# S5 tables issued behind the first half of the FFN with a narrower scratch, and two mixer gates issued before the NSA heads, in a two-block transformer kernel

## Chip, cores and metric

One core of one Trainium2 chip runs the whole program in one launch. The metric is the device time of one execution in microseconds (us), the median of several runs. Besides, one execution is recorded by the hardware profiler; its span is the time from the first to the last instruction.

## What is computed

Two transformer blocks in fp32 on 256 tokens of width 1024. Cut to what matters here:

```
first_block:                                   # x_lat [256, 1024]
    h = modulate(rmsnorm(x), shift, scale)     # shift, scale: silu(c) @ w_ada, a GEMV
    x = x + g_a * (two attentions of h) @ w_out
    h = modulate(rmsnorm(x), sh_f, sc_f)
    gate, up = split(h @ w_ffn_in, 2)          # FFN hidden 2816
    x = x + g_f * ((silu(gate) * up) @ w_ffn_out)
    x = rmsnorm(x)
second_block:
    hp = rmsnorm(x) @ w_in_2                   # u | q | kv | nsa gates | two mixer gates of 1024
    y_ssm = s5_mixer(u)                        # complex diagonal scan over 32 groups x 64 states
    y_nsa = nsa_mixer(q, kv)                   # compressed + selected + window attention, 8 heads
    merged = sigmoid(gate0) * (y_ssm @ w_proj_ssm) + sigmoid(gate1) * (y_nsa @ w_proj_nsa)
    x = x + merged @ w_out_2
    x = x + square(relu(rmsnorm(x) @ w_up)) @ w_down
s5_mixer: abar = exp(a*dt); bbar = f(abar) * b; x_t = abar * x_(t-1) + bbar u_t
          y = Re(c x) + d u;  yg = gelu(y);  out = yg * sigmoid(yg @ w_glu + b_glu)
```

Rotating the states by the phase of abar turns the complex scan into real ones. That needs cos and sin of every phase times every step: these are the tables of this study. They depend on the parameters alone, not on x.

## The kernel before, in words

**Products.** Activations lie transposed, `[128 channels, 256 tokens]` a tile, so a weight tile of 128x128 is the stationary operand and 256 (or 258) tokens stream. A product in fp32 accuracy is made of three fp32r matmuls: high part of the weight with the high part of the activation, high with low, and low with high. Weights come as `raw` buffers of 1024 KB by SP's DMA, in the order in which the program uses them; there are three such buffers, each of two halves of 128x1024. For each half ScalarE (ACT) copies `raw` to `hi`, then VectorE (DVE) makes `lo = raw - hi`. TensorE (PE) thus needs one ACT and one DVE instruction for each 24 matmuls (8 tiles times 3). `hi` and `lo` have four buffers each.

**Who orders the work.** Every operation is recorded by the class `Rec` and none is issued at once; all show line 660 (`Rec.issue`) in the profile, so the rows are read by tile names. `schedule()` is a planner with its own costs that fixes the order of the instructions of each engine; its priority is the index in the program plus `rec.shift`. An operation recorded while `rec.gate` holds another one can't be placed before that one has ended. Hardware semaphores do the rest: each engine works through its fixed order and waits where an operand isn't ready.

**FFN, first half (`ffi`).** The loop `for j in range(22)` makes for each `z` of 0, 1 a group of 24 matmuls into one PSUM bank (tags `mm` and `s` in turn), 44 groups in all, 22 pairs. A reading on DVE (`c<-mm,k_rsf` or `c<-s,k_rsf`, 128x258) and small operations follow each group; a pair ends in `hid[j]`, which is split into high and low by ACT and DVE. At j = 2, 6, 10, 14 a `gemv` (a piece of the next adaptive-norm product, `raw<-raw,k_crow`) runs on DVE and GpSimd (POOL) and keeps one `raw` buffer meanwhile. At j = 7 `s5_params()` is recorded: all S5 parameters, complex products of 128x512 and 128x256 on POOL (`c<-c,k_fr`, `k_neg`, `k_abr`, `k_abi`) and, at its end, `tables()`.

**The tables.** `tables()` writes cos and sin of 16 groups of phases for 128 steps by doubling: at level n it squares the phase (small operations of 128x16) and fills columns n to 2n from columns 0 to n by six POOL operations (three pairs: `tab<-tab,col`, `c<-tab,col`, `tab<-tab,c`), in pieces of as many groups as fit in the scratch. The scratch was `c2()`, 512 columns. First use is in the S5 scan (`c<-v,tab`) far behind.

**FFN, second half (`ffo`).** For each of 8 output tiles 66 matmuls over the 22 `hid` tiles; DVE adds the residual, splits and squares.

**Second block.** `site(name)` calls stand all along it and place pieces of other work between its own: `S5_AT` says how many steps of the S5 scan, `GATE_AT` how many mixer gates. One `gate_step()` makes one 256-wide mixer gate, two groups of 24 matmuls (`mm<-xs`), so 48 matmuls, two `hi`, two `lo`, two ACT copies and two POOL multiplications by `r12`. Seven gates are to be done before the GLU (`GATES_A`); those that the sites don't place are recorded after the last S5 steps. Site `c` stands after the compressed keys and values (`k_kcn`, `k_vcn`) and before the scores with them (`s<-k_crow,k_kcn`); `h11`, `h12`, `h13` stand behind the head pairs 1 to 3 of the second query tile, `p10` behind its first value product. Query tile 0 has 128 keys, tile 1 has 256.

Of the kernel before, what the change touches and what calls it, by code (L numbers as in the profile page):

```python
# [202 lines left out]


S5P_AT = 7
S5A_SHIFT = 600
HI_SHIFT = 30
LO_SHIFT = -30
# [5 lines left out]
POOL_A, POOL_B, POOL_N = (1,), (0,), (0, 1)  # L214

S5_AT = {"k0": 1, "k1": 1, "v": 1, "q0": 4, "q2": 1, "c": 3, "h01": 1, "h03": 2, "h13": 1}
GATE_AT = {"h11": 2, "h12": 1, "h13": 2, "p10": 1}

GEMV_AT = {"v0": (0, 1), "v2": (2, 3), "a1": (4,), "a3": (5, 6), "h0": (7,), "h1": (8, 9), "h3": (10, 11)}
GEMV_POOL = [(1,)] * 3 + [()] + [(1,)] * 2 + [(0, 1)] * 3 + [()] + [(0, 1)] * 2 + [(1,), (), (1,), (1,)]  # L220
# [452 lines left out]
def _build(ctx, tc, nc, A, out):  # L673
# [5 lines left out]
    rec = Rec(nc, BUFS)  # L679
# [11 lines left out]
    def T(tag, shape, dt=F32):  # L691
        cnt[0] += 1
        name = f"{tag}_{cnt[0]}"
        return own(sp, name, tag, shape, dt)
# [7 lines left out]
    def PS(tag, shape):  # L702
        cnt[0] += 1
        name = f"{tag}_{cnt[0]}"
        return own(pp, name, tag, shape, F32)
# [16 lines left out]
    def c1(dt=F32, n=256):  # L722
        return T("c1", [128, n], dt)

    def c2(dt=F32):
        return T("c2", [128, 512], dt)
# [8 lines left out]
    def col(name, j=0, n=1):  # L735
        a = PC[name][0]
        return pc[:, a + j:a + j + n]
# [54 lines left out]

    rec.shift = S5A_SHIFT
    ar, ai = col("ar", 0, 16), col("ai", 0, 16)
# [573 lines left out]


    def s5_params():  # L1370
        rec.gate = {hid[0].root.w[-1]}
        ACT.activation(e1, th2, AF.Sin)

        are, den, t0 = cols16(), cols16(), cols16()
        V.tensor_tensor(abr, mag, e1[:, 0], OP.mult)
        V.tensor_tensor(aim, mag, e1[:, 1], OP.mult)
        V.tensor_tensor(mag2, mag, mag, OP.mult)
        V.tensor_scalar(are, abr, 1.0, None, op0=OP.subtract)
        V.tensor_tensor(den, ar, ar, OP.mult)
        V.tensor_tensor(t0, ai, ai, OP.mult)  # L1380
        V.tensor_tensor(den, den, t0, OP.add)
        V.reciprocal(den, den)
        V.tensor_tensor(fr, are, ar, OP.mult)
        V.tensor_tensor(t0, aim, ai, OP.mult)
        V.tensor_tensor(fr, fr, t0, OP.add)
        V.tensor_tensor(fr, fr, den, OP.mult)
        V.tensor_tensor(fi, aim, ar, OP.mult)
        V.tensor_tensor(t0, are, ai, OP.mult)
        V.tensor_tensor(fi, fi, t0, OP.subtract)
        V.tensor_tensor(fi, fi, den, OP.mult)  # L1390
        V.tensor_scalar(neg[:, 0], fi, -1.0, None, op0=OP.mult)
        V.tensor_scalar(neg[:, 1], aim, -1.0, None, op0=OP.mult)
        t16 = lambda: c2().rearrange("p (a b) -> p a b", a=16)
        scm = [t16(), t16()]

        nbt = [[c2().rearrange("p (a m b) -> p a m b", a=8, m=2) for _ in range(2)] for _ in range(2)]
        scd = A["sc"].rearrange("p (a b c) -> p a b c", a=16, b=2)
        for k in range(2):
            SP.dma_start(scm[k], scd[:, :, k])
            for i in range(2):  # L1400
                o = 512 * k + 256 * i
                SP.dma_start(nbt[k][i][:, :, 1], A["sbn"][:, o:o + 256].rearrange("p (a b) -> p a b", a=8))
        ct = t16()
        frb, nfb, arb, aib, nab = (f_[:, :, None].to_broadcast([128, 16, 32]) for f_ in (fr, neg[:, 0], abr, aim, neg[:, 1]))

        def cmul(o, x, yr, yi, op0, op1, ct=ct):

            G.tensor_tensor(o[0], x[0], yr, OP.mult)
            G.tensor_tensor(ct, x[1], yi, OP.mult)
            G.tensor_tensor(o[0], o[0], ct, op0)  # L1410
            G.tensor_tensor(o[1], x[0], yi, OP.mult)
            G.tensor_tensor(ct, x[1], yr, OP.mult)
            G.tensor_tensor(o[1], o[1], ct, op1)


        cp, ca = [t16(), t16()], [t16(), t16()]
        cmul(cp, scm, frb, nfb, OP.add, OP.subtract)

        cmul(ca, cp, arb, nab, OP.subtract, OP.add)
        sb2 = [[c2() for _ in range(2)] for _ in range(2)]  # L1420
        for i in range(2):
            a8 = slice(8 * i, 8 * i + 8)
            o, x = [nbt[k][i][:, :, 0] for k in range(2)], [nbt[k][i][:, :, 1] for k in range(2)]
            cmul(o, x, arb[:, a8], aib[:, a8], OP.subtract, OP.add, ct[:, a8])
            for k in range(2):
                tp = PS("tp", [128, 512])
                for p in range(4):
                    PE.transpose(tp[:, 128 * p:128 * p + 128], nbt[k][i][:, 2 * p:2 * p + 2], ident)
                ACT.activation(sb2[k][i], tp, AF.Copy)

        dd, gd = c2().rearrange("p (a b) -> p a b", a=4), c2().rearrange("p (a b) -> p a b", a=4)
        G.memset(gd, 0.0)
        for q in range(4):
            G.tensor_scalar(dd[:, q], ident, col("ssd", q), None, op0=OP.mult)
        gp = PS("tp", [128, 4, 32])
        for q in range(4):
            for k in range(2):
                for z in range(4):
                    mm(gp[32 * z:32 * z + 32, q], nbt[k][q // 2][:, (4 * q + z) % 8, 1], cp[k][:, 4 * q + z], k == 0, k == 1)
        for z in range(4):  # L1440
            r = slice(32 * z, 32 * z + 32)
            V.tensor_tensor(gd[r, :, r], gp[r], dd[r, :, r], OP.add)


        TB = [T("tab", [128, 16, 128]) for _ in range(2)]

        def tables():
            tc_, ts_ = TB
            e2 = T("col", [128, 2, 16, 1])
            tm = T("col", [128, 16, 1])  # L1450
            pr1, pi1 = e2[:, 0], e2[:, 1]

            def square(c_, s_):
                G.tensor_tensor(pr1, c_, c_, OP.mult)
                G.tensor_tensor(tm, s_, s_, OP.mult)
                G.tensor_tensor(pr1, pr1, tm, OP.subtract)
                G.tensor_tensor(pi1, c_, s_, OP.mult)
                G.tensor_scalar(pi1, pi1, 2.0, None, op0=OP.mult)
            G.memset(tc_[:, :, 0:1], 1.0)
            G.memset(ts_[:, :, 0:1], 0.0)  # L1460
            square(e1[:, 0][:, :, None], e1[:, 1][:, :, None])
            G.tensor_copy(tc_[:, :, 1:2], pr1)
            G.tensor_copy(ts_[:, :, 1:2], pi1)
            t_ = c2()
            for lv in range(1, 7):
                n = 2 ** lv
                h_ = n // 2
                square(tc_[:, :, h_:h_ + 1], ts_[:, :, h_:h_ + 1])
                nj = min(16, 512 // n)
                for j in range(0, 16, nj):  # L1470
                    j_ = slice(j, j + nj)
                    pr, pi_ = (p[:, j_].to_broadcast([128, nj, n]) for p in (pr1, pi1))
                    t = t_[:, 0:nj * n].rearrange("p (a b) -> p a b", a=nj)
                    c_, s_, cn, sn = tc_[:, j_, 0:n], ts_[:, j_, 0:n], tc_[:, j_, n:2 * n], ts_[:, j_, n:2 * n]
                    G.tensor_tensor(cn, c_, pr, OP.mult)
                    G.tensor_tensor(t, s_, pi_, OP.mult)
                    G.tensor_tensor(cn, cn, t, OP.subtract)
                    G.tensor_tensor(sn, s_, pr, OP.mult)
                    G.tensor_tensor(t, c_, pi_, OP.mult)
                    G.tensor_tensor(sn, sn, t, OP.add)  # L1480
        tables()
        rec.gate = set()
        return sb2, cp, ca, dd, gd, TB

    hid = []
    xh_ = lambda kc: xs[kc][:, 256:514]
    xl_ = lambda kc: xs[kc][:, 0:256]
    for j in range(22):
        ts = []
        for z in range(2):  # L1490
            ps = PSR([128, 258], LIN)
            lin(ps, BASE["ffi"] + 16 * j + 8 * z, 8, xh_, xl_)
            t = T("c258", [128, 258])
            V.tensor_tensor(t, ps, rsf, OP.mult)
            V.tensor_scalar(t[:, 256:257], t[:, 257:258], t[:, 256:257], None, op0=OP.add)
            ts.append(t)
        a = c1()
        ACT.activation(a, ts[0][:, 0:256], AF.Silu, bias=ts[0][:, 256:257])
        V.scalar_tensor_tensor(a, ts[1][:, 0:256], ts[1][:, 256:257], a, op0=OP.add, op1=OP.mult)
        h_ = c2(F32R)  # L1500
        split(h_[:, 0:256], h_[:, 256:512], a)
        hid.append(h_)
        if j in (2, 6, 10, 14):
            gemv(12 + j // 4)
        if j == S5P_AT:
            sb2, cp, ca, dd, gd, TB = s5_params()

    gg = K("gg", [128, 8])
    V.tensor_tensor(gg, col("fin", 0, 8), col("n1", 0, 8), OP.mult)
# [130 lines left out]
    def site(name):  # L1640

        s5_step(S5_AT.get(name, 0))
        for _ in range(GATE_AT.get(name, 0)):
            gate_step()
# [268 lines left out]
    hid = []  # L1913
# [10 lines left out]
    for m in range(8):  # L1924
        ps = PSR([128, 256], LIN)
        lin(ps, BASE["down"] + 32 * m, 32, lambda kc: hid[kc][:, 0:256], lambda kc: hid[kc][:, 256:512])
        t_ = c1()
        for z in range(2 if m == 7 else 1):
            c = slice(128 * z, 128 * z + 128) if m == 7 else slice(0, 256)
# [19 lines left out]
```

## Time and profile before

| what | value |
|---|---|
| median of 3 runs | 803.56 us (801.42 to 803.92) |
| profiled execution, time | 800.42 us |
| profiled execution, span | 798.4 us, mean granted clock 0.985 |
| PE busy | 761.0 us, 95% of the span |
| DVE, ACT, POOL busy | 582.9, 432.4, 303.5 us |

The span is 2.0 us shorter than that execution's time, and that execution is 3.1 us below the median of the runs. PE is the engine with the least idle time; how busy the others are changes from stage to stage, so a share of the whole span says little about a stage. In the views, `[1.53 <-DVE lo L660]` behind a row means that the engine was idle for 1.53 us before it and that a `lo` on DVE ended the wait. A group such as `x24` stands for consecutive instructions of one kind.

### The profile page before, as it was taken

The page shows a single profiled execution, that of the slowest core. Times are in us where ns is not written, and L with a number is a line of the kernel's source. Part 1 is how long each engine was busy: PE and PEld are TensorE (multiplying, and loading weights), DVE is VectorE, ACT ScalarE, POOL GpSimd, SP SyncE. Part 2 cuts the span into 40 slices and gives each one's busy share as a digit, 9 for nine tenths or more (in the row PEclk, how much of TensorE's full clock was granted, in tenths as well). Part 3 has the DMA queues.
Part 4 walks back from the last instruction along what each step waited for, and adds up shares of the span by engine and source line. Part 5 has one row for each costly group of instructions (what it writes and reads, how often), then busy time and mean ns, then how long its engine had stood idle before and what let it go on. Part 6 is the DMA issues. An engine that isn't in the chain of part 4 may idle for free.

```text
span 798.4 us, 15427 instructions
## 1 busy us (share of the span) xinstructions
PE 761.0 (95%) x6063; PEld 688.7 (86%) x6063; DVE 582.9 (73%) x1156; ACT 432.4 (54%) x790; POOL 303.5 (38%) x320
## 2 busy tenths in 40 slices
PE   5998999999999898899999988999999999999997
PEld 3877875568999898889999876687999999999997
DVE  6668988787997799866677788756788655555552
ACT  5435559887754445445555323486647666654331
POOL 0013355771368959800002476685350233310000
PEclk9999999999999999999999996999999999999999
DMA  9955543445786454465576401233455555555540
GB/s 329 346 209 223 211 158 114 144 147 218 199 277 214 155 212 159 159 219 203 208 271 205 136 5 53 68 117 135 148 177 205 182 188 188 182 199 192 218 172 14
DMA packets 33994, 142.89 MB, mean 179 GB/s; under 512 B 11777, under 2 KB 15233, under 8 KB 17794
## 3 DMA queue, kind: packets, MB, share of 16 engines
q1 hardware_dynamic: 33922, 141.91, 51.0%
q8 instruction: 48, 0.79, 0.4%
q14 instruction: 24, 0.20, 0.1%
HBM read 139.53 MB, written 1.05 MB: 176 GB/s over the span
## 4 chain that ended last, share of the span: by engine, by line
PE 82%; DVE 9%; DMA 2%; ACT 2%; POOL 2%; issue 1%; SPq 0%; DVEq 0%; POOLq 0%; ACTq 0%
PE mm L660 39%; PE s L660 31%; PE tp L660 6%; DVE c L660 5%; PE la L660 4%; PE v L660 3%; DVE lo L660 3%; DMA raw<-in_ada 1%; ACT c L660 1%; DMA raw<-in_wseq 1%; DVE col L660 1%; ACT hi L660 1%; POOL c L660 1%; POOL tab L660 0%; POOL col L660 0%
## 5 line engine op out<-in xcount | busy, mean ns | idle before, releaser
L660 DVE TENSOR_TENSOR lo<-raw,hi 128x1024 fp32r<-128x1024 f32 x206 | 259.8, 1265 | 92.7 <-ACT hi L660 91.5
L660 ACT ACTIVATE hi<-raw 128x1024 fp32r<-128x1024 f32 x206 | 215.7, 1051 | 194.1 <-PE mm L660 92.4
L660 PE MATMUL mm<-xs,hi 128*128 128x256 f32 (+1 forms) x992 | 185.0, 285 | 2.3 <-ACT hi L660 1.2
L660 PEld LDWEIGHTS mm<-xs,hi 128*128 128x128 f32 x992 | 153.2, 189 | 7.3 <-issue 3.4
L660 PE MATMUL mm<-c,hi 128*128 128x256 f32 (+1 forms) x744 | 140.3, 287 | 4.7 <-DVE c L660 2.7
L660 PE MATMUL mm<-xs,lo 128*128 128x256 f32 (+1 forms) x496 | 140.7, 284 | 2.0 <-DVE lo L660 2.0
L660 PEld LDWEIGHTS mm<-c,hi 128*128 128x128 f32 x744 | 113.7, 188 | 13.8 <-DVE c L660 4.4
L660 PE MATMUL s<-xs,hi 128*128 128x256 f32 (+1 forms) x672 | 125.2, 286 | 0.0
L660 PE MATMUL s<-c,hi 128*128 128x256 f32 (+1 forms) x676 | 120.6, 280 | 1.1 <-ACT hi L660 1.1
L660 PE MATMUL mm<-c,lo 128*128 128x256 f32 (+1 forms) x372 | 105.3, 284 | 1.3 <-DVE lo L660 1.2
L660 PEld LDWEIGHTS s<-c,hi 128*128 128x128 f32 x676 | 103.5, 188 | 2.7 <-ACT hi L660 1.3
L660 PEld LDWEIGHTS s<-xs,hi 128*128 128x128 f32 x672 | 104.8, 191 | 0.5
L660 PE MATMUL s<-xs,lo 128*128 128x258 f32 (+1 forms) x336 | 95.9, 285 | 5.0 <-DVE lo L660 5.0
L660 PEld LDWEIGHTS mm<-xs,lo 128*128 128x128 f32 x496 | 93.8, 189 | 4.3 <-DVE lo L660 2.6
L660 PE MATMUL s<-c,lo 128*128 128x256 f32 x338 | 94.2, 279 | 0.0
L660 ACT ACTIVATE c<-c 128x256 fp32r<-128x256 f32 (+4 forms) x141 | 61.5, 448 | 52.0 <-DVE c L660 48.9
L660 POOL TENSOR_TENSOR raw<-raw,k_crow 128x1024 f32<-128x1024 f32 x18 | 46.2, 2566 | 108.7 <-DMA raw<-in_ada 100.9
L660 DVE TENSOR_TENSOR c<-c,c 128x256 fp32r<-128x256 f32 (+2 forms) x115 | 67.3, 598 | 19.8 <-POOL c L660 15.7
L660 POOL TENSOR_TENSOR c<-c 128x256 f32<-128x256 f32 x40 | 41.6, 1039 | 92.6 <-ACT c L660 80.9
L660 PEld LDWEIGHTS mm<-c,lo 128*128 128x128 f32 x372 | 69.7, 188 | 3.1 <-DVE lo L660 1.7
L660 PEld LDWEIGHTS s<-xs,lo 128*128 128x128 f32 x336 | 64.3, 191 | 6.1 <-DVE lo L660 6.0
L660 PEld LDWEIGHTS s<-c,lo 128*128 128x128 f32 x338 | 63.5, 188 | 0.4
(257 smaller groups left out, 1140.9 us busy)
## 6 DMA issues: line engine op xcount, KB each, us to landing
raw<-in_wseq SPq DMA_DIRECT2D x102, 1024.0 KB, 4.9
raw<-in_ada SPq DMA_DIRECT2D x20, 1024.0 KB, 5.1
tab<-in_ada SPq DMA_DIRECT2D x4, 1024.0 KB, 7.1
c<-in_w SPq DMA_DIRECT2D x8, 256.0 KB, 8.6
k_X<-in_x SPq DMA_DIRECT2D x4, 256.0 KB, 4.1
raw<-in_wseq SPq DMA_DIRECT2D x2, 512.0 KB, 8.0
tab<-in_ctx SPq DMA_DIRECT2D x4, 256.0 KB, 10.5
out<-c SPq DMA_DIRECT2D x7, 128.0 KB, 1.7
```

Of the source, the lines that this page charges most:

```text
L660: getattr(self.real[o.eng], o.fn)(*[val(x) for x in o.args], **{k: val(x) for k, x in o.kw.items()})
```

## The change

The tables are recorded after the loop over the 22 pairs and are gated on `hid[14]` (TAB_GATE), where they were recorded inside the loop and gated on `hid[0]`. Their scratch is `c1()`, 256 columns instead of 512, so the pieces of the two last levels hold half as many groups and there are twice as many: 6 operations become 12 at one level, 12 become 24 at the next, 18 POOL instructions more in all. In the second block `GATE_AT` gets two gates at site `c` and one instead of two at `h11`; the seventh gate, which was recorded behind the last S5 steps, is now among those that sites place.

```diff
+PAR_GATE, TAB_GATE = 0, 14
...
-GATE_AT = {"h11": 2, "h12": 1, "h13": 2, "p10": 1}
+GATE_AT = {"c": 2, "h11": 1, "h12": 1, "h13": 2, "p10": 1}
...
     def s5_params():
-        rec.gate = {hid[0].root.w[-1]}
+        rec.gate = {hid[PAR_GATE].root.w[-1]}
...
-            t_ = c2()
+            t_ = c1()
             for lv in range(1, 7):
                 n = 2 ** lv
                 h_ = n // 2
                 square(tc_[:, :, h_:h_ + 1], ts_[:, :, h_:h_ + 1])
-                nj = min(16, 512 // n)
+                nj = min(16, 256 // n)
                 for j in range(0, 16, nj):
...
-        tables()
         rec.gate = set()
-        return sb2, cp, ca, dd, gd, TB
+        return sb2, cp, ca, dd, gd, TB, tables
...
         if j == S5P_AT:
-            sb2, cp, ca, dd, gd, TB = s5_params()
+            sb2, cp, ca, dd, gd, TB, s5_tables = s5_params()
+
+    rec.gate = {hid[TAB_GATE].root.w[-1]}
+    s5_tables()
+    rec.gate = set()
```

The planner then places everything anew. On POOL, before, where the S5 parameters begin: `tab` tiles are the tables, `col` tiles the squared phases, `c_545`, `c_546` belong to the complex products.

```order
L660 MEMSET c_563_2554 128x512
L660 MEMSET tab_2561 128x16
L660 MEMSET tab_2565 128x16
L660 TENSOR_SCALAR c_562_2584<-k_cst,k_pc 128x128 x4
L660 TENSOR_TENSOR col_2656<-k_e_161 128x16
L660 TENSOR_TENSOR col_2660<-k_e_161 128x16
L660 TENSOR_TENSOR c_545_2563<-c_545_2563,k_abr 128x8x32
```

On POOL in the changed kernel, where the tables begin; `raw_3045` and `raw_3453` are the POOL halves of the GEMV pieces of j = 10 and 14.

```order
L662 TENSOR_TENSOR raw_3045<-raw_3045,k_crow 128x1024
L662 TENSOR_TENSOR c_549_2993<-c_548_2607,k_abr 128x256
L662 TENSOR_TENSOR c_548_2607<-c_548_2607,c_549_2993 128x8x32
L662 TENSOR_TENSOR raw_3453<-raw_3453,k_crow 128x1024
L662 MEMSET tab_3698 128x16
L662 MEMSET tab_3703 128x16
L662 TENSOR_TENSOR col_3707<-k_e_161 128x16
```

The whole of the tables has moved behind all complex products and behind the last GEMV piece; nothing of POOL's own is queued behind them until the second block. SP's order of transfers is the same in both kernels.

On DVE, before, near the end of `ffi` (readings of groups 36 to 38 of the 44):

```order
L660 TENSOR_TENSOR lo_3892<-raw_3685,hi_3792 128x1024
L660 TENSOR_TENSOR c_679_3910<-s_3794,k_rsf 128x258
L660 TENSOR_SCALAR c_679_3910<-c_679_3910 128x1
L660 SCALAR_TENSOR_TENSOR c_680_3882<-c_679_3910,c_680_3882 128x256
L660 TENSOR_TENSOR c_681_3929<-c_680_3882,c_681_3929 128x256
L660 TENSOR_TENSOR c_685_3948<-mm_3898,k_rsf 128x258
L660 TENSOR_SCALAR c_685_3948<-c_685_3948 128x1
L660 TENSOR_TENSOR lo_3953<-raw_3751,hi_3834 128x1024
L660 TENSOR_TENSOR lo_3959<-raw_3751,hi_3866 128x1024
L660 TENSOR_TENSOR lo_3970<-raw_3820,hi_3900 128x1024
```

On DVE in the changed kernel, the same part of the loop:

```order
L662 TENSOR_TENSOR lo_3854<-raw_3638,hi_3831 128x1024
L662 TENSOR_TENSOR c_676_3877<-s_3829,k_rsf 128x258
L662 TENSOR_SCALAR c_676_3877<-c_676_3877 128x1
L662 SCALAR_TENSOR_TENSOR c_677_3849<-c_676_3877,c_677_3849 128x256
L662 TENSOR_TENSOR lo_3899<-raw_3692,hi_3874 128x1024
L662 TENSOR_TENSOR c_678_3896<-c_677_3849,c_678_3896 128x256
L662 TENSOR_TENSOR c_682_3920<-mm_3872,k_rsf 128x258
L662 TENSOR_SCALAR c_682_3920<-c_682_3920 128x1
L662 TENSOR_TENSOR lo_3936<-raw_3692,hi_3915 128x1024
```

Before, no `lo` stands between the readings of two successive groups here and four follow in a row; after, one `lo` stands between every two readings. Counted over the loop, a `lo` stands three groups before the group that needs it at best; before, this lead falls to none at groups 21, 37, 42 and 43, and is one at 30 to 33, 35, 36 and 41; after, it falls to none at group 25 alone and is three from group 30 to the end.

On PE, before, at the compressed keys: `s<-k_crow,k_kcn` are their scores (`k_crow` holds the queries there), `mm<-xs` are matmuls of gates, `v` and the last rows before them belong to S5.

```order
L660 MATMUL tp_5915<-c_940_5911,k_bones 128x16
L660 MATMUL tp_5917<-c_924_5618,c_937_5896 16x64 x2
L660 MATMUL s_5929<-k_crow,k_kcn 32x256 x4
L660 MATMUL s_5936<-k_crow,k_kcn 32x256 x4
L660 MATMUL s_5950<-k_cst,c_957_5944 128x128 x2
L660 MATMUL s_5956<-c_848_5237,k_crow 128x128
```

On PE in the changed kernel, the same place:

```order
L662 MATMUL tp_5934<-c_924_5636,c_937_5904 16x64 x2
...
L662 MATMUL mm_5769<-xs_4988,hi_5569 128x256 x2
L662 MATMUL mm_5769<-xs_4988,lo_5914 128x256
L662 MATMUL s_5972<-k_crow,k_kcn 32x256 x4
L662 MATMUL s_5981<-k_crow,k_kcn 32x256 x4
L662 MATMUL v_1021_5987<-k_cst,c_555_3350 128x128
L662 MATMUL v_1021_5987<-k_cst,c_557_3435 128x128
L662 MATMUL mm_5843<-xs_4309,lo_5936 128x256
L662 MATMUL mm_5843<-xs_4416,hi_5648 128x256 x2
```

Gate matmuls now stand between the small products of the compressed keys and their scores (20 of them, at "..."), and more behind. Counted from the start of the second block, 20 more of them than before stand ahead of these scores, 58 more ahead of the first value product of query tile 0, and 42 more ahead of the last one of query tile 1; behind the last score of the heads 144 are left, where 192 were. Three fewer S5 scans or products with the tables and two more `lo` stand ahead of `k_kcn` on DVE.

## Rows read from the trace of the kernel before

**Rows 1.** The page: span; busy time, its share and instructions of each engine.

```profile
span 798.4 us, 15427 instructions
PE 761.0 (95%) x6063; PEld 688.7 (86%) x6063; DVE 582.9 (73%) x1156; ACT 432.4 (54%) x790; POOL 303.5 (38%) x320
```

**Rows 2.** Windows: stretch, length, PE, PEld, DVE, ACT, POOL busy, clock, DMA share, GB/s.

```profile
203.00:262.00 59.00, 59.00 (x489) 58.94 (x489) 51.97 (x105) 32.87 (x49) 38.60 (x56) 1.00 0.77 248
262.00:304.00 42.00, 39.27 (x370) 38.65 (x369) 37.79 (x57) 20.41 (x32) 33.31 (x34) 0.96 0.48 174
304.00:347.00 43.00, 36.91 (x293) 35.26 (x293) 36.36 (x50) 18.84 (x26) 31.19 (x25) 1.00 0.45 155
347.00:376.00 29.00, 29.00 (x258) 29.00 (x257) 20.21 (x27) 15.44 (x21) 0.00 (x0) 1.00 0.63 225
...
465.00:483.00 18.00, 14.91 (x188) 12.08 (x188) 17.05 (x43) 4.17 (x10) 13.47 (x23) 1.00 0.00 1
483.00:502.00 19.00, 17.16 (x124) 12.02 (x124) 16.96 (x72) 7.22 (x29) 14.63 (x19) 0.55 0.20 60
502.00:527.00 25.00, 24.37 (x145) 16.54 (x144) 14.57 (x83) 15.63 (x52) 16.42 (x26) 1.00 0.23 83
527.00:562.00 35.00, 35.00 (x300) 29.62 (x298) 22.91 (x43) 25.12 (x53) 24.19 (x25) 1.00 0.35 121
```

**Rows 3.** Chain of waits in order of time: start, duration, what.

```profile
259.12 2.91 PE s L660 x24
...
268.88 4.34 PE s L660 x22
```

**Rows 4.** PE's timeline, 264 to 348 us: start, duration, instruction, idle time before it.

```profile
268.88 0.58 PE L660 MATMUL s<-xs,lo 128*128 128x258 f32 x1 [2.36 <-DVE lo L660]
...
303.96 0.40 PE L660 MATMUL mm<-xs,hi 128*128 128x258 f32 x2
...
309.25 0.39 PE L660 MATMUL s<-xs,lo 128*128 128x258 f32 x1 [1.53 <-DVE lo L660]
...
347.09 0.28 PE L660 MATMUL mm<-c,lo 128*128 128x256 f32 x1
```

**Rows 5.** DVE by groups, 215 to 262 us: count, busy time, mean ns of one.

```profile
L660 DVE TENSOR_TENSOR lo<-raw,hi 128x1024 fp32r<-128x1024 f32 x15 | 18.4, 1235 | 0.1
```

**Rows 6.** DVE by groups, 264 to 278 us.

```profile
L660 DVE TENSOR_TENSOR lo<-raw,hi 128x1024 fp32r<-128x1024 f32 x5 | 7.9, 1598 | 0.0
```

**Rows 7.** DVE by groups, 304 to 336 us.

```profile
L660 DVE TENSOR_TENSOR lo<-raw,hi 128x1024 fp32r<-128x1024 f32 x10 | 18.5, 1874 | 0.0
```

**Rows 8.** DVE by groups, 347 to 376 us.

```profile
L660 DVE TENSOR_TENSOR lo<-raw,hi 128x1024 fp32r<-128x1024 f32 x13 | 15.9, 1223 | 7.4 <-ACT hi L660 7.4
```

**Rows 9.** POOL by groups, 304 to 337 us.

```profile
L660 POOL TENSOR_TENSOR tab<-tab,c 128x512 f32<-128x512 f32 x6 | 11.5, 1916 | 0.5
L660 POOL TENSOR_TENSOR tab<-tab,col 128x512 f32<-128x512 f32 x6 | 9.4, 1566 | 0.0
L660 POOL TENSOR_TENSOR c<-tab,col 128x512 f32<-128x512 f32 x6 | 8.2, 1358 | 0.0
```

**Rows 10.** POOL's timeline, 295 to 305 us: a level in 256-column pieces, the next one's start.

```profile
295.37 0.80 POOL L660 TENSOR_TENSOR tab<-tab,col 128x256 f32<-128x256 f32 x1
...
300.09 1.61 POOL L660 TENSOR_TENSOR tab<-tab,c 128x256 f32<-128x256 f32 x1
...
304.45 1.05 POOL L660 TENSOR_TENSOR tab<-tab,col 128x512 f32<-128x512 f32 x1
```

**Rows 11.** Chain of waits, 480 to 530 us.

```profile
486.84 1.12 PE s L660 x16
...
490.33 1.36 PE mm L660 x5
```

**Rows 12.** PE's timeline, 557 to 562 us.

```profile
557.82 1.27 PE L660 MATMUL tp<-c,c 128*32 128x127 f32 x34
...
561.79 0.39 PE L660 MATMUL mm<-c,hi 128*128 128x256 f32 x2
```

## The prediction

> **What bounds the kernel now.** I first read the page for the engine with the least idle time: PE, 761.0 of 798.4 us [rows 1]. So only about 37 us of idle time and whatever runs at the lower clock can be won at all, and the question is in which stage they lie. The windows tell [rows 2]. The start of the FFN's first half (203 to 262 us) and its second half (from 347 us) have no idle PE. Two stretches have: 262 to 347 us, with 2.7 and 6.1 us of it, and the sparse attention with the S5 steps, 465 to 527 us, with 3.1, 1.8 and 0.6 us, where besides the granted clock is 0.55 for 19 us, that is near the lower of its two levels (1.2 of 2.4 GHz). The change touches both.
>
> In the first stretch a group of 24 matmuls takes 2.91 us when nothing is late [rows 3], 0.121 us a matmul. The last twelve groups of the FFN's first half take from 303.96 to 347.09, 43.1 us, where twelve times 2.91 is 34.9: 8.2 us are lost. The timeline names the releaser, a `lo` of DVE [rows 4]. Why is DVE late there? The same `lo` takes 1.235 us from 215 to 262, where POOL is 65% busy with mostly small table operations and complex products; 1.598 from 264 to 278 beside 256-column products of POOL; 1.874 from 304 to 336 beside its 512-column table operations; 1.223 from 347 where POOL does nothing [rows 2, 5 to 8]. So POOL's long operations with two inputs stretch DVE, and DVE is 85% busy there (36.36 of 43). And the order leaves no room: the lead of `lo` is one group for most of 30 to 36 and none at 37, 42 and 43.
>
> **The tables, cost step by step.** Before, the last two levels were 18 operations of 512 columns, 11.5 + 9.4 + 8.2 = 29.1 us [rows 9]. After, they are 36 of 256 columns. Six of these took from 295.37 to 301.70, 6.33 us, 1.06 each [rows 10], so 36 take 38.0: 9 us more on POOL. The gate is the split of pair 14, whose matmuls end two groups ahead of 303.96 [rows 4], near 298; its reading, SiLU and split follow, so I let the tables start near 302. Four lower levels take at most 6.33 each, 25.3, and seven squares at most what one takes here, 301.70 to 304.45, 2.75, so 19.3: all in all at most 83, with an end by 385 us. As the lowest levels are shorter I estimate 73 and an end near 375. The S5 scan, which first reads them, is far behind; so the added POOL time itself costs nothing, its cover being those idle 70 us or more of POOL. What it may cost is DVE time.
>
> *304 to 347 us.* The large operations leave this stretch for its most part; from 302 to about 331 the small ones run, beside which `lo` is as in the first stretch (excess 0.01 us), and then 256-column ones (excess 1.598 - 1.223 = 0.375). For the ten `lo` that is between 0.1 and 3.75 us of DVE time in place of 6.5 (ten times 0.651). I take the last four, 1.5 us, which the lead of three groups in the new order (8.7 us) mostly covers, and charge 1.0: 7.2 of the 8.2 us come back. Bounds 4.4 and 8.2.
>
> *The earlier stall.* At 268.88 PE had waited 2.36 us for a `lo`, and the 22 matmuls then took 4.34 us instead of 22 x 0.121 = 2.66 at a lower clock [rows 3, 4]: 4.0 us. Lead none moves from group 21 to group 25, behind the same readings and beside the same kind of POOL products. I count 0: at best 4.0 is won, at worst 1 lost.
>
> *The second half from 347 us.* It had an idle POOL, and DVE idle for 29 - 20.21 = 8.8 us of 29 [rows 2]. Now 256-column operations run there to about 375. Thirteen `lo` times 0.375 are 4.9 us, which fits; at the 512-column rate, 13 x 0.651 = 8.5, it only just fits, and other operations with two inputs would overflow it. I take the shape that runs, and charge 0.5; bounds 0 and 3.
>
> FFN together: 7.2 + 0 - 0.5 = 6.7 us won.
>
> **The two gates, step by step.** Behind the last head score, where PE is 35.00 of 35 busy [rows 2], 48 matmuls go: 48 x 0.121 = 5.8 us won if PE keeps setting the pace there. They come back ahead, with others that the planner pulls along: 58 more before the first value product of query tile 0. The idle 3.1 + 1.8 + 0.6 = 5.5 us of PE take 45 of them at full clock; 13 are left, 1.5 us lost. Four new DVE and ACT operations each come with two gates; only two more `lo` stand ahead of `k_kcn`, 2.4 us, minus three small S5 operations, and DVE is 17.05 of 18 busy there: I charge 1.2 (bounds 0 and 2.4). POOL's earlier multiplications fall where it is 13.47 of 18 busy: nothing, behind them wait S5 products that have 4.5 us of room. The gate matmuls between small products keep PE at work, so the clock should stay at its upper level more of the time from 483 to 502; that can't return more than DVE's idle time there, 19 - 16.96 = 2.0 us, and I take half, 1.0 won. At the end, the last S5 transposes end at 559.09 and gate matmuls cover the 2.7 us to the GLU at 561.79 while ACT makes the gelu [rows 12]. With 48 fewer left a part of this cover goes: 1.0 lost (0 to 2.7). Sum: 5.8 - 1.5 - 1.2 + 1.0 - 1.0 = 3.1 us won; bounds 7.8 won, and the loss of the third rival.
>
> **Sum.** 6.7 + 3.1 = 9.8 us. The profiled execution's span would go from 798.4 to 788.6, its time from 800.4 to 790.6; the median lies 3.1 us above that execution before, and taken off it the sum gives 803.6 - 9.8 = 793.8 us.
>
> **Rivals.** *The FFN gains, the gates nothing.* For it: DVE is 34.0 of 37 us busy from 465 to 502 [rows 2], so PE's idle time there is time spent waiting for DVE, and whatever PE is given in it, the chain of small operations takes as long, with two `lo` added. Against: PE is full behind it. 803.6 - 6.7 = 796.9.
>
> *POOL blocks DVE in the second half.* If each `lo` from 347 us on waited for a whole 256-column operation, 1.06 us, 13 would lose 13.8 us where 8.8 are idle: 5.0 lost, in place of 0.5. 793.8 + 4.5 = 798.3. Against: beside operations of 1.6 us (29.1 / 18) the excess was 0.65 each, not 1.6. The Trainium skill, "SBUF — State Buffer", section "Who interferes with whom", speaks for this rival and against the change: a DVE instruction with two SBUF inputs contends with a GpSimd one that reads SBUF, by an exclusive lock on a shared port pair. The trace agrees that the two slow each other, by 0.65 us and not by a whole instruction; by the lock alone the time would be this rival's.
>
> *The gates delay the attention.* PE works in order, so each gate matmul between two steps of a chain that goes from PE to DVE and back delays the next step unless the operand was late anyway. At this stage five gate matmuls took 1.36 us in the chain [rows 11], 0.272 each; 58 on the chain are 15.8 us. The first scores with the compressed keys, at 486.84, then come late, all behind follows, and what goes behind the last score is no gain, because S5 and the values set the end there. 6.7 - 15.8 = 9.1 us slower, 812.7. It decides in favour of slower when over 9.1 us, 33 of the 58, stay on the chain. For it: the clock of 0.55 there; against: 5.5 us of idle PE that these matmuls can fill.
>
> *The tables are not the reason.* If the late `lo` of groups 32 to 43 came from what else DVE has queued (readings, GEMV pieces) and not from the tables, the new order stalls again, at other groups. Of the 8.2 us, say 2 come back and 3.1 from the gates: 798.5. Against: the row of `lo` that changes from 1.874 to 1.223 us when POOL falls silent.
>
> **How the numbers follow.** Forecast 0.60, FFN alone 0.15, POOL blocks 0.07, not the tables 0.09, gates delay 0.09. The runs of this kernel lie within 0.3% (2.4 us) of their median, and that much tells a change from none. Of the forecast 0.59 is faster, of the second 0.13, of the third 0.05, of the fourth 0.05: 0.82 faster. Gates delay is slower, 0.09. The rest, 0.09, is the same. The likeliest case by itself runs from about 788 (the gates at their 7.8 and a little of the earlier stall) to 798. The range takes in the other faster cases above and, below, 4.0 of the earlier stall with 7.8 of the gates and 8.2: 786 to 802.5; left out are the slower case, half of "the same" and little below, about 0.15.
>
> **What would show it.** In the changed kernel's profile: `lo` from 304 to 331 us near 1.24 and then near 1.6, with POOL busy to about 375; PE from the start of group 32 to the end of the first half near 36 us, not 43; one wait for a `lo` of 2 to 3 us near 275; no idle PE in the second half. PE's idle time between the S5 matmuls and the first value product below 4 us, and the granted clock of that stretch above 0.55; the GLU starting about 9.8 us earlier than 561.79. I am wrong if PE shows waits for DVE from 347 to 376 (third case), or if the scores with the compressed keys, seen from the end of the FFN, come later than before by more than 3 us.

## The result, and the profile after

The changed kernel takes 792.43 us in the median of 4 runs (791.63 to 794.38), the kernel before, measured beside it, 802.49 (800.39 to 803.92): a ratio of 0.9889, 95% interval 0.9857 to 0.9922. The span of the profiled execution fell from 798.4 to 790.6 us. The page of the changed kernel, as in [rows 1]:

```profile
span 790.6 us, 15465 instructions
PE 756.9 (96%) x6063; PEld 685.6 (87%) x6063; DVE 585.2 (74%) x1156; ACT 433.2 (55%) x790; POOL 308.9 (39%) x338
```

The windows of the changed kernel at the stretches of [rows 2], with the same columns:

```profile
203.00:262.00 59.00, 57.73 (x474) 57.26 (x473) 54.52 (x106) 32.63 (x48) 22.92 (x20) 1.00 0.71 232
262.00:304.00 42.00, 40.83 (x397) 40.31 (x396) 39.71 (x64) 22.19 (x34) 29.76 (x40) 1.00 0.63 225
304.00:347.00 43.00, 43.00 (x363) 43.00 (x362) 37.72 (x54) 23.22 (x30) 41.31 (x60) 1.00 0.55 197
347.00:376.00 29.00, 29.00 (x259) 29.00 (x258) 21.69 (x25) 15.26 (x23) 15.26 (x15) 1.00 0.51 183
...
465.00:483.00 18.00, 13.21 (x132) 10.98 (x129) 14.79 (x40) 2.09 (x6) 10.03 (x17) 0.81 0.17 59
483.00:502.00 19.00, 19.00 (x159) 14.26 (x159) 13.87 (x85) 10.53 (x42) 13.35 (x22) 1.00 0.16 57
```

From 304 to 347 us PE has no idle time left, where it had 6.1 us, and the table operations of 256 columns run beside it and into the second half of the FFN. These are the same stretches of time, not of work: behind the FFN the changed kernel is about 9 us further on. In the attention the picture only shifted: the lower clock has moved from 483 to 502 us to the stretch before it, and PE there is idle for 4.8 us, not 3.1; from 483 to 502 it has no idle time left, where it had 1.8 us.

**Where the time went, by stage.** Three landmarks on PE's timeline cut the span: the first matmul of the FFN, the first matmul of the second block behind the FFN, and the last instruction. Of the kernel before, then of the changed one:

```profile
203.40 0.40 PE L660 MATMUL mm<-xs,hi 128*128 128x258 f32 x2
...
406.53 0.39 PE L660 MATMUL mm<-xs,hi 128*128 128x256 f32 x2
```

```profile
203.33 0.40 PE L662 MATMUL mm<-xs,hi 128*128 128x258 f32 x2
...
397.17 0.39 PE L662 MATMUL mm<-xs,hi 128*128 128x256 f32 x2
```

The FFN, taken to the end of its last matmul, went from 203.3 to 194.0 us: 9.3 won. The rest, to the span's end, went from 391.7 to 393.3: 1.6 lost. Up to the FFN nothing changed in these two executions. In others the time up to it differs: a further run of the same changed kernel reached its first FFN matmul at 208.75 us, and its span was 797.0. The windows of that run:

```profile
0.00:30.00 30.00, 21.13 (x126) 14.19 (x126) 18.08 (x87) 16.44 (x27) 1.45 (x7) 0.89 0.91 342
...
60.00:100.00 40.00, 36.85 (x215) 30.29 (x214) 32.37 (x70) 20.56 (x46) 11.37 (x9) 0.91 0.58 216
```

The granted clock falls there in stretches in which it is 1.00 in the execution of 790.6 us. From the first FFN matmul on the two differ by 1.0 us in 588. Over all profiled executions of this study that matmul starts between 203.0 and 209.3 us, in kernels with the same instructions before it. So the experiments below are read from it on, each from one profiled execution: "FFN" is the time from it to the end of the FFN's last matmul (203.3 before, 194.0 after), "rest" from there to the end of the span (391.7 and 393.3).

### The profile page after: what moved, and what is told of

Read it like the earlier page. It is cut to its first block, busy times and chain, and to the rows that moved or that the text cites. A ratio compares the mean times of both kernels' runs of the same rounds, so it can differ in the third digit from the quotient of the medians.

```text
span 790.6 us, 15465 instructions
## 1 busy us (share of the span) xinstructions
PE 756.9 (96%) x6063; PEld 685.6 (87%) x6063; DVE 585.2 (74%) x1156; ACT 433.2 (55%) x790; POOL 308.9 (39%) x338
## 3 DMA queue, kind: packets, MB, share of 16 engines
HBM read 139.53 MB, written 1.05 MB: 178 GB/s over the span
## 4 chain that ended last, share of the span: by engine, by line
PE 86%; DVE 7%; ACT 3%; DMA 2%; issue 1%; POOL 0%; SPq 0%; DVEq 0%; ACTq 0%; POOLq 0%
PE mm L662 41%; PE s L662 33%; PE tp L662 6%; DVE c L662 4%; PE la L662 3%; PE v L662 3%; ACT c L662 2%; DVE lo L662 1%; DMA raw<-in_wseq 1%; DVE col L662 1%; DMA raw<-in_ada 1%; ACT hi L662 1%; DVE raw L662 0%; DVE k_adc L662 0%; SPq L662 0%
## 5 line engine op out<-in xcount | busy, mean ns | idle before, releaser
L662 DVE TENSOR_TENSOR lo<-raw,hi 128x1024 fp32r<-128x1024 f32 x206 | 265.9, 1294 | 84.1 <-ACT hi L662 82.9
L662 DVE TENSOR_TENSOR c<-c,c 128x256 fp32r<-128x256 f32 (+2 forms) x115 | 63.5, 564 | 22.6 <-POOL c L662 15.7
L662 POOL TENSOR_TENSOR c<-c,c 128x128 f32<-128x128 f32 (+2 forms) x72 | 48.2, 692 | 51.3 <-DVE c L662 50.5
```

Source lines behind the costliest of these rows:

```text
L662: getattr(self.real[o.eng], o.fn)(*[val(x) for x in o.args], **{k: val(x) for k, x in o.kw.items()})
```

## The experiments

**Each half of the change alone.** The tables alone, with the gates as before:

```diff
-GATE_AT = {"c": 2, "h11": 1, "h12": 1, "h13": 2, "p10": 1}
+GATE_AT = {"h11": 2, "h12": 1, "h13": 2, "p10": 1}
```

> Tables as in the changed kernel, the gates at their places of before. Theory A, read from the changed kernel's trace (the FFN gives 9.4 us, the gates cost about 2 by the end): 9 to 10 us faster than before, so a span near 789 and as fast as or 1 to 2 us faster than the changed kernel. Theory B, the sum of the prediction (FFN 6.7, gates 3.1): 6.7 us faster than before, about 3 slower than the changed kernel. Both: the second half of the FFN ends near 397 us if A holds, near 400 if B.

Measured: 795.0 us, ratio to before 0.9931 (0.9911 to 0.9951). FFN 194.0, rest 394.2. The FFN's 9.3 us are the tables' alone. The rest is 2.5 us longer than before though the change touches none of its operations, only the planner's order of them; theory A is right on the FFN and missed this.

The gates alone, on the kernel before, with the line of `GATE_AT` that the changed kernel has:

> The gates alone at their new places, tables as before. Theory A: 1 to 3 us slower than before (the scores with the compressed keys come about 4.7 us later than the FFN's end says, about 2.5 of it come back behind the last score). Theory B: 3 us faster than before. The FFN's end is near 406.7 us in both.

Measured: 801.99 us, ratio 1.001 (0.9987 to 1.0033): no change. FFN 201.4, rest 393.4. The FFN's 1.9 us are not the gates': DVE works through the FFN in the order of before, and 1.4 of them come behind the wait of [rows 4] at 268.88 us. PE waits there for the same `lo` in this run, 2.35 us, but the granted clock does not fall behind it. The windows of the kernel before, then of this run, with the columns of [rows 2]:

```profile
266.00:278.00 12.00, 9.62 (x66) 9.41 (x67) 10.45 (x13) 3.29 (x7) 11.76 (x12) 0.86 0.40 132
```

```profile
266.00:278.00 12.00, 9.28 (x76) 8.86 (x75) 10.61 (x14) 3.10 (x6) 11.69 (x10) 1.00 0.25 89
```

Six profiled kernels of this study have that wait. Behind it the clock fell in four, to 0.86 in this window, and in two it did not. So about 1.4 us between the FFN times of two executions can be the clock alone.

Theory B's 3 us are not there. Up to the scores with the compressed keys the way from the FFN's end is 85.2 us where it was 80.1, and 3.3 us come back behind. The changed kernel shows what stands in that way. Its chain of waits there, then its DVE, then the last step of the keys on the DVE of the kernel before:

```profile
478.26 4.01 PE mm L662 x20
482.27 0.59 PE s L662 x16
```

```profile
475.36 1.21 DVE L662 TENSOR_TENSOR lo<-raw,hi 128x1024 fp32r<-128x1024 f32 x1
...
477.46 1.32 DVE L662 TENSOR_TENSOR lo<-raw,hi 128x1024 fp32r<-128x1024 f32 x1
...
478.91 0.22 DVE L662 SCALAR_TENSOR_TENSOR k_kcn<-col,k_pc,c 128x16 f32<-128x16 f32 x1
```

```profile
486.58 0.21 DVE L660 SCALAR_TENSOR_TENSOR k_kcn<-col,k_pc,c 128x16 f32<-128x16 f32 x1
```

The keys are ready at 479.1, but the 20 gate matmuls that stand ahead of the scores have begun at 478.26 and take 4.0 us, 0.20 each, with the granted clock of that stretch at 0.81: 3.1 us of wait. Before there was none: the keys were ready at 486.8, and the scores began at 486.84. Seen from the FFN's end the keys are ready at 81.8 us in the changed kernel and in this run, where it was 80.1 before. These 1.7 us and the wait (3.1 us, in this run 3.3) are the whole delay of the scores, 4.7 and 5.0 us. Two `lo`, 2.5 us, now lie between the small steps that make the keys, but the step ahead of the first `lo` is late by 0.9 us already; how much of the 1.7 us is theirs is not shown.

**One gate there in place of two.**

```diff
-GATE_AT = {"c": 2, "h11": 1, "h12": 1, "h13": 2, "p10": 1}
+GATE_AT = {"c": 1, "h11": 2, "h12": 1, "h13": 2, "p10": 1}
```

> The changed kernel with one gate ahead of the scores with the compressed keys and two at h11. If each gate there costs about 2.7 us up to these scores and gives about 3.2 back behind them (half of what two do), the scores come 82 us after the FFN's end (79.4 with none, 84.9 with two) and the total lies within 1 us of the changed kernel. If what the planner makes of each arrangement decides, not the number of gates, the two stretches don't lie between those of none and two, and the total is over 2 us away in either direction.

Measured: 792.48 us, ratio 0.9893 (0.9865 to 0.9921). The scores with the compressed keys come 83.3 us after the FFN's end, between 79.4 and 84.9, but from them to the end of the last score it takes 45.8 us, with none 42.5 and with two 39.7. The rest is 394.3, against 394.2 with none and 393.3 with two. So the first stretch goes by the number of gates and the second does not; the sum stays within 1 us. The changed kernel itself, measured beside this one:

> The changed kernel itself, beside the others of this call. By both theories as before: ratio 0.988 to 0.991; FFN 194.0.

Measured: 795.8 us, ratio 0.994 (0.9921 to 0.9959); FFN 194.0, rest 394.2. Its profiled execution, 798.78 us, is the slowest of 12 (from 791.89), and it is the one that reached its FFN at 208.75 us. So its late start explains 5.4 of the 6.4 us between this execution and that of the result, but where the others lose, and with them the median, is not shown.

**Narrow or wide, early or late.** The change moves the tables and narrows them. First the narrow scratch at the old place:

```diff
-            t_ = c2()
+            t_ = c1()
...
-                nj = min(16, 512 // n)
+                nj = min(16, 256 // n)
```

> The tables at their place of before, with the scratch of 256 columns (36 wide operations for 18). Width theory (narrower operations stretch DVE less): lo beside them near 1.5 us in place of 1.87, the FFN from its first matmul to its last 2 to 3 us shorter than the 203.3 of before. Pool theory (the narrow scratch matters only because it comes from another pool, which lets the tables start late): FFN within 1 us of 203.3, or longer, since the tables take about 9 us more beside the first half; total within 0.3% of before or slower.

Measured: 794.92 us, ratio 0.992 (0.9891 to 0.9948). FFN 194.3, rest 393.3. The move isn't needed for the most part of the FFN's gain: 9.0 of 9.3 us come with the narrow pieces at the old place. About 1.4 of the 9.0 are the clock of this execution, which stayed at 1.00 behind the wait at 268.66 us; a run below has the same tables and 7.6. The pool theory falls here, and the width theory gave a third of what came. Its DVE by groups from 304 to 336 us, beside 256-column tables, against 1874 ns in [rows 7]:

```profile
L660 DVE TENSOR_TENSOR lo<-raw,hi 128x1024 fp32r<-128x1024 f32 x13 | 19.7, 1519 | 0.0
```

Then the wide pieces at the new place, with the scratch from the pool that it had before (the lines above the other way round, on the changed kernel):

> The changed kernel with the scratch of 512 columns again: 18 wide table operations instead of 36. If the width of the operations is what stretches DVE (lo 1.87 us beside them, against 1.5), PE waits for a lo again before 347 us or in the second half: 1 to 3 us slower than the changed kernel. If only the place counts, because the order has a lead of three groups and DVE idles in the second half: within 0.5 us of it.

Measured: 817.5 us, ratio 1.0228 (1.0195 to 1.0262): 16 us slower than before. Neither theory said that. FFN 194.0, rest 418.1. POOL's timeline of this run:

```profile
390.48 1.27 POOL L662 TENSOR_TENSOR c<-tab,col 128x32 f32<-128x32 f32 x1 [90.47 <-PE s L662]
```

POOL waited for 90 us for PE: the 512-column scratch comes from the pool `c2`, whose buffers the `hid` tiles hold until the second half of the FFN has read them. The tables then run into the second block, where the scores with the compressed keys come 108.0 us after the FFN's end, not 84.9. So this run says nothing of the width; it says that the late place needs a scratch from another pool, which is what the narrow one is. With a 512-column buffer of its own:

```diff
-            t_ = c1()
+            t_ = T("tscr", [128, 512])
...
-                nj = min(16, 256 // n)
+                nj = min(16, 512 // n)
...
-    BUFS = dict(c1=20, c2=32, ...
+    BUFS = dict(tscr=1, c1=18, c2=32, ...
```

> The changed kernel with a scratch of 512 columns in a buffer of its own, so that the tables needn't wait for one that the FFN's hidden tiles hold (two c1 buffers fewer make the room; the second block may be planned otherwise for that). Width theory: PE waits for lo beside the 512-column operations, the FFN takes 195 to 197 us where the changed kernel takes 194.0. Place theory: 194.0 to 194.5, and the tables start near 302, not at 390.

Measured: 794.09 us, ratio 0.9907 (0.9873 to 0.9942). FFN 195.0, rest 390.4. The first half is as quick as with narrow pieces (134.2 us); the second half loses 0.9, of it 0.63 in one wait of PE for a `hi` of ACT. DVE from 347 to 376 us in this run, whose FFN began 5.9 us later, then in the changed kernel:

```profile
L662 DVE TENSOR_TENSOR lo<-raw,hi 128x1024 fp32r<-128x1024 f32 x10 | 17.7, 1804 | 0.0
```

```profile
L662 DVE TENSOR_TENSOR lo<-raw,hi 128x1024 fp32r<-128x1024 f32 x11 | 14.8, 1342 | 7.5 <-ACT hi L662 7.5
```

Beside wide pieces DVE has no idle time before its `lo` there, beside narrow ones it still has 7.5 us. Width costs 0.9 us at the late place, so both theories are near; place and width each give most of the gain by itself.

**Contention or order.** Wide operations of POOL can cost in two ways: they stretch DVE when they run, and the planner, which counts on that, puts `lo` late. Two runs take one of them away each, from the kernel before. First its order is kept, and POOL writes constants of the same size in place of the wide table operations:

```diff
             o = self.ops[i]
+            wide = o.eng == "G" and o.fn == "tensor_tensor" and _free(o.args[0]) == 512 and any(
+                isinstance(x, View) and x.root.tag == "tab" for x in o.args)
+            if wide:
+                self.real["G"].memset(val(o.args[0]), 0.5)
+                continue
```

> The kernel before with its order of instructions unchanged; each of the 18 table operations of 512 columns is replaced by a POOL memset of the same destination, so these parts of the tables hold a constant and the S5 output is another. A memset reads nothing. Contention theory (POOL's reads stretch DVE's operations with two inputs): lo from 304 to 336 us falls from 1.87 to about 1.23, the waits for lo go, groups 32 to 43 take 36 to 38 us instead of 43: 5 to 7 us faster than before. Order theory (the planned order leaves lo no lead, whatever POOL does): lo gets shorter but PE still waits, 40 us or more: 0 to 3 us faster.

Measured: 797.42 us, ratio 0.997 (0.9953 to 0.9986). FFN 200.0, 3.3 us won. Its DVE from 304 to 336 us, and a row of its PE:

```profile
L665 DVE TENSOR_TENSOR lo<-raw,hi 128x1024 fp32r<-128x1024 f32 x10 | 11.9, 1216 | 0.0
```

```profile
336.33 0.39 PE L665 MATMUL mm<-xs,lo 128*128 128x258 f32 x1 [1.18 <-DVE lo L665]
```

A `lo` is as short as beside an idle POOL, 1.22 us, and PE still waits. Then the other way round: the same operations as before, with a planner that takes the 18 wide ones as free of contention, so that only the order changes:

```diff
         o.dur, o.port = self.cost(eng, m, args, kw, reads)
+        if eng == "G" and m == "tensor_tensor" and _free(out) == 512 and any(x.root.tag == "tab" for x in reads + writes):
+            o.port = False
```

> The kernel before, with 512-column table operations at their place, but planned as if these 18 operations did not share anything with DVE, so only the order of instructions changes; what runs on the chip is the same set of operations. Order theory (most of the loss was that the planned order leaves lo no lead): the first half of the FFN takes 134 to 137 us in place of 143.85, though lo beside the tables stays near 1.87 us. Contention theory (the stretched DVE can't keep up in any order): 140 us or more.

Measured: 798.33 us, ratio 0.9963 (0.9939 to 0.9987). FFN 197.6, of it 137.7 for the first half: 5.7 us won. DVE from 304 to 340 us, and the longest of the two waits for a `lo` that PE has left behind 304 us:

```profile
L662 DVE TENSOR_TENSOR lo<-raw,hi 128x1024 fp32r<-128x1024 f32 x12 | 20.7, 1727 | 0.0
```

```profile
310.62 0.39 PE L662 MATMUL s<-xs,lo 128*128 128x258 f32 x1 [1.54 <-DVE lo L662]
```

A new order alone gives back 5.7 us, no contention alone 3.3, both in executions whose clock fell behind the early wait as before. Both theories hold, the order's part being the larger. The two are not shares of one sum: the narrow pieces at the old place give 7.6 us where the clock fell, so some of the loss goes with either. No run takes both away at once.

**The change without its move**, narrow pieces at the old place and the gates as in the changed kernel:

> The change without its move: tables at their place of before, with the 256-column scratch, and the gates as in the changed kernel. If the narrow scratch alone is enough in the FFN and the gates give nothing: FFN 194.3, second block 392.5 to 394, the total within 1.5 us of the changed kernel. If the move matters beside it: 2 us or more slower than the changed kernel.

Measured: 800.18 us, ratio 0.9999 (0.9974 to 1.0023): nothing is left. FFN 195.7, rest 398.0. Neither half of the expectation held. The FFN gain is 7.6 us, 1.4 smaller than with the gates at their old places, and that is the clock: up to the wait of 2.36 us, here at 268.49 us, both runs agree within 0.01 us; from 266 to 278 us the granted clock is 0.86 here and was 1.00 there. The rest is 4.7 us longer than with the gates at their old places (393.3), where beside the late tables it was the same or 0.9 shorter (394.2 without, 393.3 and 394.2 with). The scores with the compressed keys come 85.3 us after the FFN's end, 5.7 later than without the two gates there; 1.1 us come back up to the end of the last score, and behind it nothing (271.1 and 271.0), though some 48 gate matmuls fewer are left there.

**A version to beat both.** The shorter rest of the run with its own scratch, tried by itself on the changed kernel:

```diff
-    BUFS = dict(c1=20, c2=32, ...
+    BUFS = dict(c1=18, c2=32, ...
```

> The changed kernel with 18 buffers c1 in place of 20, which was part of the run with a 512-column scratch of its own. FFN 194.0 us. If the shorter second block of that run (390.4 us from the FFN's end to the span's end, 393 in the changed kernel) came with the buffers: about 390.5 here, 2 to 3 us faster than the changed kernel. If it came by the planner's chance with the whole arrangement: 392 to 395, no gain.

Measured: 791.26 us, ratio 0.9885 (0.9851 to 0.9919), span 787.9. FFN 194.2, rest 390.4. It repeats the 390.4 and is 2.7 and 3.7 us shorter than the two profiled executions of the changed kernel from the first FFN matmul on. By the ratios to before (0.9889 and 0.994 for the changed kernel, measured at other times) it is no slower; they don't tell it apart for certain.

## Why the prediction was right, and where its terms were not

The forecast was 793.8 us, measured were 792.43, inside the range. By the spans the sum was 9.8 us and 7.8 came. It is right as a total because two terms missed to opposite sides, the FFN by 2.6 us and the gates by 4.7, and in that there is luck. The prediction also named a sign of being wrong: the scores with the compressed keys more than 3 us later, seen from the FFN's end. They come 4.7 us later (84.9 against 80.1), so its account of the gates failed by its own sign. The same kernel measured again gave 795.8, inside the range as well.

**The FFN, 6.7 forecast, 9.3 measured.** The mechanism held, as experiments with the gates at their old places show. The term for 304 to 347 us was put at 7.2 with bounds to 8.2; PE is 43.00 of 43 us busy there. The last twelve groups take 35.0 us to the end of their last matmul, where they took 43.3. But these 43.3 us, and so the 8.2 lost of the prediction, held four matmuls of the FFN's second half, which PE did between its waits:

```profile
338.01 0.40 PE L660 MATMUL mm<-c,hi 128*128 128x256 f32 x2
...
343.56 0.51 PE L660 MATMUL s<-c,hi 128*128 128x256 f32 x2 [1.09 <-ACT hi L660]
```

They now come later, 0.45 us, so 7.8 us are won. `lo` is not the 1.24 us forecast for the small operations: its group from 304 to 336 us in the changed kernel reads

```profile
L662 DVE TENSOR_TENSOR lo<-raw,hi 128x1024 fp32r<-128x1024 f32 x12 | 17.8, 1482 | 0.4 <-ACT hi L662 0.4
```

so DVE was stretched more than assumed. The tables began at 291.5 us, not near 302, and their 256-column operations at 314.8, not near 331:

```profile
291.47 0.17 POOL L662 MEMSET tab<- 128x16 f32 x2
...
314.78 0.62 POOL L662 TENSOR_TENSOR tab<-tab,col 128x256 f32<-128x256 f32 x1
```

The lead of three groups covered it: the order carried the larger part, as the two separating runs show. The forecast named both, but drew nearly all of its 7.2 us from the shorter `lo` and let the lead cover only the last four. "The earlier stall", counted at 0, gave the rest, 1.5 us: group 32 begins 99.1 us after the first matmul, not 100.6. It was replaced, as forecast, but by two short waits, without the lower clock that followed the long one of [rows 4]:

```profile
261.55 0.39 PE L662 MATMUL s<-xs,lo 128*128 128x258 f32 x1 [0.90 <-DVE lo L662]
...
281.18 0.39 PE L662 MATMUL s<-xs,lo 128*128 128x258 f32 x1 [1.17 <-DVE lo L662]
```

In all seven profiled executions with late tables the clock stays at 1.00 here, while behind the long wait it fell in four of six; so most of the 1.5 us is won only against an execution in which it falls.

The second half was charged 0.5. It takes 59.90 us from the first half's last matmul to its own, where it took 59.45; that is the four matmuls, so it lost nothing. The table operations of 256 columns were forecast at 1.06 us, with an end near 375; from 300 to 380 us POOL shows

```profile
L662 POOL TENSOR_TENSOR tab<-tab,c 128x256 f32<-128x256 f32 x14 | 15.9, 1132 | 1.1
L662 POOL TENSOR_TENSOR tab<-tab,col 128x256 f32<-128x256 f32 x14 | 14.9, 1066 | 0.0
L662 POOL TENSOR_TENSOR c<-tab,col 128x256 f32<-128x256 f32 x14 | 12.3, 880 | 0.0
```

1.03 each, and the last ends at 362.7 us. The rival in which POOL blocks DVE in the second half fell: `lo` there is 1.342 us, 0.12 more than beside an idle POOL, where a whole operation would have added 1.06.

**The gates, 3.1 forecast, 1.6 lost with all that the planner changed behind the FFN.** The step that failed is "the idle 5.5 us of PE take 45 of them at full clock". Idle time of PE in this chain, which goes to and fro between PE and DVE, is not free for work that stands ahead of the chain's next step: 20 gate matmuls took 4.0 us, 0.20 each where the forecast had 0.121, 3.1 of them after the operand was there; and the operand itself came 1.7 us later. The forecast's 1.2 and its share of the 1.5 for this came to 4.7 us up to the scores. Behind these 3.2 us came back, 2.6 of them behind the last score of the heads, where 5.8 were forecast. That is the third rival in part, with its mechanism at its place, and a price far below its 15.8 us. The second rival, gates worth nothing, describes it best: alone they gave no change, beside the late tables 0 to 0.9 won in the rest, beside the early narrow ones 4.7 lost.

**What stays open.** The rest takes 390.4 to 398.0 us in the runs whose tables end within the FFN, while its operations are the same but for the gates' places and two buffers. Each arrangement of what goes before makes the planner choose another order; which step of it makes the 3 to 5 us was not tried.

## What to carry to other kernels

Before moving an operation off an engine, look at the order that a planner makes because of it: here a new order gave back more (5.7 us) than taking the contention away (3.3 us). Idle time in a chain that alternates between two engines was no room for other work that stands ahead of the chain's next step in the queue; behind that step it was not tried. Before a difference of 1 or 2 us between two traces is put down to an edit, compare the granted clock of the stretch, and count the same instructions on both sides. And a scratch is also a claim on a pool: a late operation that takes its scratch from a pool held by live tiles waits for them, 90 us here.

## What the runs showed of the hardware

A `lo` (DVE, two inputs) takes 1.87 us in the mean beside POOL operations of 512 columns that read two operands [rows 7]. With memsets of that width in their place it takes 1.22, and the two that ran wholly beside memsets took 1.22 and 1.21. So POOL's reading does it, not its writing. The Trainium skill, "SBUF — State Buffer", section "Who interferes with whom", says so: such a DVE instruction contends with a GpSimd one that reads and not with one that only writes. The runs agree in this.

The prediction took the mean excess of 0.65 us as a sign that a `lo` doesn't wait for a whole POOL operation. Single rows of the kernel before read otherwise, three of POOL and the `lo` among them:

```profile
304.45 1.05 POOL L660 TENSOR_TENSOR tab<-tab,col 128x512 f32<-128x512 f32 x1
...
306.77 1.34 POOL L660 TENSOR_TENSOR tab<-tab,c 128x512 f32<-128x512 f32 x1
308.07 2.03 POOL L660 TENSOR_TENSOR tab<-tab,col 128x512 f32<-128x512 f32 x1
```

```profile
306.90 2.30 DVE L660 TENSOR_TENSOR lo<-raw,hi 128x1024 fp32r<-128x1024 f32 x1
```

The `lo` begins 0.13 us behind a POOL operation that ends at 308.11, and ends at 309.20, 1.1 us later: nearly its whole 1.22 us lie behind that operation. The next POOL operation begins at 308.07 and takes 2.03 us, where the same shape took 1.05 without a `lo`: it ends 0.9 us after the `lo`. So here one waits for the other almost to its end, and POOL bears a part of the price. The mean of `lo` alone shows only DVE's part of it.

The time to the first FFN matmul differs by up to 6 us between executions with the same instructions up to it, with the granted clock at 0.89 and 0.91 in stretches of a late one, 1.00 in an early one. In the two profiled executions of the changed kernel the time from there on repeats within 1.0 us of 588, where the medians of its two measurements were 792.4 and 795.8. It need not repeat so well in a kernel with a long wait of PE: behind one of 2.36 us the granted clock fell in one execution (0.86 from 266 to 278 us) and not in another with the same order up to there (1.00), which was 1.4 us.
